# A second queue for the kept results of the first gate/up stage

## The chip, the cores and the metric

The kernel runs on one core of a Trainium2 chip. The metric is the device time of one execution in microseconds; the time before is the median of three runs. All data is float32. TensorE is called PE in the profile, its weight loads PEld, VectorE DVE, ScalarE ACT, GpSimd POOL and SyncE SP. Entries with a q (SPq, ACTq) belong to an engine's instruction queue, where its DMAs are issued, in order.

## What is computed

One decoder layer over 2048 rows of 1024: a mixing sub-layer (sliding-window attention beside a convolution group, then an output projection), and a SwiGLU channel mixer with 2816 inner channels. The change lies in the channel mixer:

```python
hn = rms_norm(h, ffn_pre_g)
ff = (jax.nn.silu(hn @ w_gate) * (hn @ w_up)) @ w_down
h = h + rms_norm(ff, ffn_post_g)
```

## The kernel before

The 2048 rows are worked on as four tiles of 512 rows. The channel mixer takes two tiles at a time: first the pair `ws = (0, 1)`, later the pair `ws = (2, 3)`. For each pair, `stage_pre` and `stage_p1` make the gate and up products and `stage_p2` the down product. The three stages of the first pair stand before those of the second, and between and beside them run lanes of other work: the attention of the last tile, the convolution taps (`fc@C`, VectorE), the output projection and norms (`stage_w`, `norm_w`), the preparation of operands (`stage_h_plain`, `stage_h_sums`) and, beside the first pair's `stage_p1`, differences of the down weights (`stage_tsums`, lines 1072 to 1086), which load and store through SP's queue and compute on VectorE.

The gate/up product is a two-by-two block product done by a scheme of seven products instead of eight. `STEPS` (line 869) lists them: index 0 is A11 times B11, 1 is S1 times T1, 2 is S2 times T2, 3 is A12 times B21, 4 is S3 times T3, 5 is S4 times B22, 6 is A22 times T4. The A operands are weight blocks and their sums (`sums`, line 971, on VectorE), the B operands activations and their sums. Every operand is split into a high and a low part, so that a product is twelve matmuls of 128 x 128 by 128 x 512 (`product`, line 874). The split of a weight block takes a copy on ScalarE (line 792) and a subtraction (line 796; on VectorE throughout the first pair).

`MATS` (line 872) lists 44 row blocks of weights, gate and up in turn. Of these, the first `PRE` (20 for the first pair, 16 for the second) have two of their seven products done early, in `stage_pre`, since the operands B11 and B21 need only the first tile of the pair. `stage_pre` runs over q from 0 to 2 x PRE: in the first half product A11 B11 of block m is copied out of PSUM by ScalarE into an `fa` tile (line 941) and stored to a DRAM array `keeps` (line 942, on ScalarE's queue, 256 KB each). In the second half the kept result is fetched (`fetch`, line 900, issued at q for q + 2), copied by ScalarE into a PSUM bank (`seed`, line 915, one product ahead) and product A12 B21 is accumulated onto it; the outcome is final for one quarter of the output and goes through silu or the product with the gate. The first eight q of the first pair are run inside `stage_w(1)`, the rest after it.

`stage_p1` then runs over all row blocks m. For a block with m < PRE the steps are 1, 2, 4, 5, 6, so it has five products (nst = 5, j counts them); the others have all seven. At j = 0 the kept result of A11 B11, loaded a second time, is copied into the PSUM bank "B" (line 1026), onto which step 2 accumulates at j = 1. Inside block m, `sums(m + 1)` are written at j = nst - 4, `fetch(m + 1)` at j = nst - 2 (line 1066) and the weight loads `loads(m + 2)` at j = nst - 1.

Buffers: `gb` has two, used by the kept results in both stages and by `y5` (line 1036) in `stage_p1`; `fa` has four, `raw` two, `chl` five; the PSUM tag `mm` has four banks. GpSimd does, in this stretch of the first pair, the attention's selects (line 494), the row norms' small operations (lines 153 to 156) and twelve of the low parts of T1, T3 and T4 in `stage_h_sums` (line 796).

The program's order is not what the engines follow to the letter: a scheduler takes the instructions by priority, in the order written, with a simulated time line, gives each tile a buffer when one is free, and fixes one order for each engine's queue at build time. At run time each queue goes in that order and every instruction waits for its own producers.

Of the kernel before, what the change touches and what calls it, by code (L numbers as in the profile page):

```python
# [37 lines left out]
def layer_kernel(ctx, tc, x, xT, cols, rows, sinks, relb, onehot, w_in, w_pw, w_out, w_gate, w_up, w_down, out):  # L38
    nc = tc.nc
# [15 lines left out]
    def t_(tag, shape, dt=F32):  # L55
        return sb.tile(list(shape), dt, tag=tag, name=nm(tag), bufs=BUFS[tag])
# [4 lines left out]
    def f2(tag, shape=(P, T)):  # L61
        return t_(tag, shape)

    def hl(tag):
        return t_(tag, (P, 2, T), F32R)
# [725 lines left out]
    def split_f(x, w):  # L791
        act(w[:, 0], x, AF.Copy)  # L792
        return w

    def lo(x, w, on_pool):
        (ptt if on_pool else vtt)(w[:, 1], x, w[:, 0].bitcast(F32), ALU.subtract)
# [77 lines left out]
    def product(o, w, op, first):  # L874
        n = 0
        for k in range(4):
            ks = slice(k * P, (k + 1) * P)
            for a, b in ((0, 0), (0, 1), (1, 0)):
                mat(o, w[:, a, ks], op[k][:, b], start=first and n == 0, stop=n == 11, skip_group_check=not first)
                n += 1  # L880

    def stage_pre(ws, ops, mid, keep, q0=0, q1=None):
        PRE = PRES[ws[0]]
        q1 = q1 or 2 * PRE
        L = f"F{ws[0]}"
        raws = {}
        wops = {}
        kept = {}

        def load(q):  # L890
            if q < q1 and q % 2 == 0:
                lab[0] = L
                half, m = divmod(q, PRE)
                raw = t_("raw", (P, 2, T))
                for j in range(2):
                    src, pr = MATS[m + j]
                    nc.sync.dma_start(raw[:, j], src[2 * pr][:, half * T : (half + 1) * T])
                    raws[q + j] = raw[:, j]

        def fetch(q):  # L900
            if PRE <= q < q1:
                lab[0] = L
                kept[q] = f2("gb")
                nc.sync.dma_start(kept[q], keep[q - PRE])

        def split(q):
            if q < q1:
                lab[0] = L
                raw = raws.pop(q)
                wops[q] = split_f(raw, hl("w"))  # L910
                lo(raw, wops[q], ws[0] and q % 2 == 1)

        seeded = {}

        def seed(q):
            if PRE <= q < q1:
                lab[0] = L
                seeded[q] = mm()
                act(seeded[q], kept.pop(q), AF.Copy)  # L919

        load(q0)
        load(q0 + 2)
        for q in range(q0, q0 + 3):
            split(q)
        for q in range(q0, q1):
            half, m = divmod(q, PRE)
            started.add(f"P{ws[0]}.{q}")
            bn = "B21" if half else "B11"
            if len(ops.get(bn, ())) < 4:
                lh.until(f"{bn}.{ws[0]}")  # L930
            split(q + 3)
            load(q + 4)
            fetch(q + 2)
            lab[0] = L
            seed(q + 1)
            lab[0] = L
            o = seeded.pop(q) if half else mm()
            product(o, wops.pop(q), ops[bn], not half)
            if not half:
                u = f2("fa")  # L940
                act(u, o, AF.Copy)
                nc.scalar.dma_start(keep[m], u)
            else:
                if MATS[m][0] is w_gate:
                    sg = f2("fa")
                    act(sg, o, AF.Silu)
                else:
                    vtt(sg, sg, o, ALU.mult)
                    nc.sync.dma_start(mid[0, MATS[m][1]], sg)
            yield 2.76  # L950

    def stage_p1(ws, ops, mid, keep):
        PRE = PRES[ws[0]]
# [7 lines left out]
        def loads(m):  # L961
            if m < len(MATS):
                lab[0] = L
                src, pr = MATS[m]
                r0 = t_("raw", (P, 2, T))
                nc.sync.dma_start(r0, src[2 * pr].rearrange("p (a b) -> p a b", a=2))
                r1 = t_("chl", (P, 2, T))
                nc.sync.dma_start(r1, src[2 * pr + 1].rearrange("p (a b) -> p a b", a=2))
                raws[m] = dict(A11=r0[:, 0], A12=r0[:, 1], A21=r1[:, 0], A22=r1[:, 1])

        def sums(m):
            if m < len(MATS):
                lab[0] = L
                r = raws[m]
                s12 = t_("chl", (P, 2, T))
                r["S1"], r["S2"] = s12[:, 0], s12[:, 1]
                vtt(r["S1"], r["A21"], r["A22"], ALU.add)
                vtt(r["S2"], r["S1"], r["A11"], ALU.subtract)
                s34 = t_("chl", (P, 2, T))
                r["S3"], r["S4"] = s34[:, 0], s34[:, 1]  # L980
                vtt(r["S3"], r["A11"], r["A21"], ALU.subtract)
                vtt(r["S4"], r["A12"], r["S2"], ALU.subtract)

        wops = {}
        kept = {}

        def split(q):
            if q < len(todo):
                m, j, i, n = todo[q]
                lab[0] = L  # L990
                wops[q] = split_f(raws[m][STEPS[i][1]], hl("w"))
                lo(raws[m][STEPS[i][1]], wops[q], ws[0] and i in POOL_LO)

        def fetch(m):
            if m < PRE:
                lab[0] = L
                kept[m] = f2("gb")
                nc.sync.dma_start(kept[m], keep[m])

        loads(0)  # L1000
        sums(0)
        for q in range(AHEAD):
            split(q)
        loads(1)
        fetch(0)
        sg = {}
        for q, (m, j, i, nst) in enumerate(todo):
            pre = m < PRE
            gate = MATS[m][0] is w_gate
            pr = MATS[m][1]  # L1010
            split(q + AHEAD)
            lab[0] = L
            which, an, bn = STEPS[i]
            if len(ops.get(bn, ())) < 4:
                lh.until(f"S{ws[0]}")
                lab[0] = L
            if j == 0:
                bk = {}
                if not gate:
                    blocks = {}  # L1020
                    if pre:
                        blocks[3] = f2("fa")
                        nc.sync.dma_start(blocks[3], mid[0, pr])
                if pre:
                    bk["B"] = mm()
                    act(bk["B"], kept.pop(m), AF.Copy)  # L1026
            first = which not in bk
            if first:
                bk[which] = mm()
            o = bk[which]  # L1030
            product(o, wops.pop(q), ops[bn], first)
            if i == 0:
                bk["B"] = mm()
                act(bk["B"], o, AF.Copy)
            elif i == 1:
                y5 = f2("gb")
                act(y5, o, AF.Copy)
            elif i == 2:
                x2 = f2("at")
                act(x2, o, AF.Copy)  # L1040
            else:
                v = {4: y5, 5: x2}.get(i, o)
                if v is not o:
                    vtt(v, v, o, ALU.add)
                if gate:
                    s = f2("fa")
                    act(s, v, AF.Silu)  # L1047
                    sg[i] = s
                else:
                    s = sg.pop(i)  # L1050
                    vtt(s, s, v, ALU.mult)
                    blocks[i] = s
                    if i in (3, 4, 6):
                        nc.sync.dma_start(mid[{3: 0, 4: 4, 6: 1}[i], pr], s)
                    if i == 5:
                        a11, a22, a21 = blocks[3], blocks[4], s
                        for to, o_, p_, op, q_ in ((5, a22, a21, ALU.add, a22), (3, a21, a11, ALU.subtract, a21),
                                                   (2, a11, a22, ALU.subtract, a11)):
                            (ptt if ws[0] else vtt)(o_, p_, q_, op)
                            nc.sync.dma_start(mid[to, pr], o_)  # L1060
                    if i == 6:
                        (ptt if ws[0] else vtt)(s, s, blocks[3], ALU.subtract)
                        nc.sync.dma_start(mid[6, pr], s)
            if j == nst - 4:
                sums(m + 1)
            if j == nst - 2:
                fetch(m + 1)
            if j == nst - 1:
                loads(m + 2)
            yield 2.76  # L1070
# [337 lines left out]
    ws, ops = (0, 1), {}  # L1408
# [12 lines left out]
    ws, ops = (2, 3), {}  # L1421
# [76 lines left out]
```

## Time and profile before

| what | us |
|---|---|
| median of 3 runs | 1991.65 |
| lowest and highest run | 1988.4, 1992.08 |
| profiled execution, device time | 1988.67 |
| its span, first to last instruction | 1986.6 |

The granted TensorE clock of that execution was 0.992 of full speed. The DMAs that the change touches, from the profile's list of issues:

```profile
gb@F<-keeps SPq DMA_DIRECT2D x72, 256.0 KB, 3.9
...
keeps<-fa@F ACTq DMA_DIRECT2D x36, 256.0 KB, 5.0
```

The last figure is the median time in microseconds from issue to landing. The rows are for both pairs: 40 of the 72 loads and 20 of the 36 stores belong to the first. A name like `gb@F` is a tile's tag with the stage in which it was made: A and B mixing, C convolution, W output projection, H operand preparation, F gate and up, G down, and G also the differences of the down weights. The bracket behind a line of the timeline holds the idle time before the instruction and what ended it.

### The profile page before, as it was taken

The page shows a single profiled execution, that of the slowest core. Times are in us where ns is not written, and L with a number is a line of the kernel's source. Part 1 is how long each engine was busy: PE and PEld are TensorE (multiplying, and loading weights), DVE is VectorE, ACT ScalarE, POOL GpSimd, SP SyncE. Part 2 cuts the span into 40 slices and gives each one's busy share as a digit, 9 for nine tenths or more (in the row PEclk, how much of TensorE's full clock was granted, in tenths as well). Part 3 has the DMA queues.
Part 4 walks back from the last instruction along what each step waited for, and adds up shares of the span by engine and source line. Part 5 has one row for each costly group of instructions (what it writes and reads, how often), then busy time and mean ns, then how long its engine had stood idle before and what let it go on. Part 6 is the DMA issues. An engine that isn't in the chain of part 4 may idle for free.

```text
span 1986.6 us, 26669 instructions
## 1 busy us (share of the span) xinstructions
PE 1930.2 (97%) x8730; PEld 1542.3 (78%) x8730; DVE 1460.2 (73%) x2578; ACT 955.2 (48%) x1878; POOL 336.4 (17%) x415
## 2 busy tenths in 40 slices
PE   8999999998999999899999999989999999999997
PEld 6777767776777778778888778768888888888886
DVE  5999969986875898888658975766666665455557
ACT  5455454436737633334355466556634433345443
POOL 4011111003121200000000110144423332311003
PEclk9999999999999999999999999989999999999999
DMA  8797757669659867885477788797844542466664
GB/s 312 253 316 234 228 176 242 213 198 306 203 191 353 290 216 237 285 267 181 154 236 251 266 302 282 270 315 244 289 149 165 170 164 81 143 232 194 210 196 144
DMA packets 229403, 454.56 MB, mean 229 GB/s; under 512 B 22632, under 2 KB 48400, under 8 KB 229264
## 3 DMA queue, kind: packets, MB, share of 16 engines
q1 hardware_dynamic: 211024, 426.64, 64.5%
q10 hardware_dynamic: 18240, 26.22, 3.6%
q8 instruction: 69, 1.13, 0.2%
q14 instruction: 70, 0.57, 0.1%
HBM read 331.65 MB, written 121.12 MB: 228 GB/s over the span
## 4 chain that ended last, share of the span: by engine, by line
PE 43%; DMA 10%; DVE 9%; issue 3%; POOL 2%; ACT 2%; SPq 1%; DVEq 0%; ACTq 0%; POOLq 0%
PE mm@F L85 29%; PE mm@G L85 12%; DVE fc@C L94 2%; PE tr@W L85 2%; DMA gb@F<-keeps 1%; DVE hl@G L94 1%; DMA mids<-fa@F 1%; DMA fa@G<-mids 1%; DMA td<-fc@G 1%; DVE w@F L94 1%; DMA fc@G<-w_down 1%; DMA wx@G<-w_down 1%; DVE fa@F L94 1%; DVE chl@F L94 1%; DMA mixT<-fc@C 1%
## 5 line engine op out<-in xcount | busy, mean ns | idle before, releaser
L94 DVE SCALAR_TENSOR_TENSOR fc@C<-glu@C,colt,fc@C 128x512 f32<-128x512 f32 x480 | 356.5, 760 | 2.9
L85 PE MATMUL mm@F<-hl@H,w@F 128*128 128x512 f32 x1056 | 253.0, 390 | 3.3 <-ACT mm@F L919 2.0
L85 PE MATMUL mm@G<-hl@G,hl@G 128*128 128x512 f32 x924 | 232.6, 397 | 11.2 <-ACT hl@G L792 7.7
L85 PEld LDWEIGHTS mm@F<-hl@H,w@F 128*128 128x128 f32 x1056 | 197.5, 188 | 46.3 <-ACT mm@F L919 3.7
L85 PEld LDWEIGHTS mm@G<-hl@G,hl@G 128*128 128x128 f32 x924 | 173.0, 190 | 51.7 <-ACT hl@G L792 9.0
L85 PE MATMUL mm@A<-hl@A,w@A 128*128 128x512 f32 x840 | 206.5, 395 | 4.2 <-ACT w@A L127 1.9
L792 ACT ACTIVATE w@F<-chl@F 128x512 fp32r<-128x512 f32 x220 | 135.4, 625 | 142.1 <-PE mm@F L85 131.5
L85 PE MATMUL mm@G<-w@G,hl@G 128*128 128x512 f32 x876 | 199.4, 389 | 0.0
L85 PEld LDWEIGHTS mm@G<-w@G,hl@G 128*128 128x128 f32 x876 | 164.4, 188 | 34.1
L85 PEld LDWEIGHTS mm@A<-hl@A,w@A 128*128 128x128 f32 x840 | 155.4, 188 | 42.2 <-ACT w@A L127 2.6
L94 DVE TENSOR_TENSOR w@F<-chl@F,w@F 128x512 fp32r<-128x512 f32 x198 | 144.8, 735 | 35.9 <-ACT w@F L792 35.3
L85 PE MATMUL mm@F<-ql@H,w@F 128*128 128x512 f32 x528 | 128.4, 391 | 9.2 <-ACT mm@F L1026 5.0
L85 PE MATMUL mm@F<-mid@H,w@F 128*128 128x512 f32 x528 | 131.7, 396 | 0.0
L85 PE MATMUL mm@F<-p@H,w@F 128*128 128x512 f32 x528 | 129.4, 390 | 0.0
L85 PE MATMUL mm@F<-x@H,w@F 128*128 128x512 f32 x528 | 125.7, 391 | 0.0
L85 PEld LDWEIGHTS mm@F<-ql@H,w@F 128*128 128x128 f32 x528 | 98.8, 188 | 31.6 <-ACT mm@F L1026 6.4
L494 POOL TENSOR_SCALAR_AFFINE_SELECT p@B<-p@B 128x512 f32<-128x512 f32 x62 | 57.6, 938 | 374.0 <-ACT p@B L492 372.7
L85 PEld LDWEIGHTS mm@F<-mid@H,w@F 128*128 128x128 f32 x528 | 100.0, 190 | 21.9 <-ACT fa@F L1047 0.5
L85 PEld LDWEIGHTS mm@F<-p@H,w@F 128*128 128x128 f32 x528 | 99.5, 188 | 21.0 <-ACT at@F L1040 0.2
L85 PEld LDWEIGHTS mm@F<-x@H,w@F 128*128 128x128 f32 x528 | 98.6, 188 | 21.5 <-issue 0.8
L127 ACT ACTIVATE w@A<-raw@A 128x512 fp32r<-128x512 f32 x110 | 67.4, 625 | 93.5 <-PE mm@A L85 54.8
L94 DVE TENSOR_TENSOR w@G<-raw@G,w@G 128x512 fp32r<-128x512 f32 x73 | 51.5, 705 | 68.1 <-ACT w@G L792 66.8
(302 smaller groups left out, 3300.6 us busy)
## 6 DMA issues: line engine op xcount, KB each, us to landing
mids<-fa@F SPq DMA_DIRECT2D x154, 256.0 KB, 2.8
raw@A<-w_in SPq DMA_DIRECT2D x55, 512.0 KB, 4.7
w@A<-lo_in SPq DMA_DIRECT2D x84, 256.0 KB, 3.6
fc@G<-mids SPq DMA_DIRECT2D x77, 256.0 KB, 3.5
fa@G<-mids SPq DMA_DIRECT2D x75, 256.0 KB, 4.6
gb@F<-keeps SPq DMA_DIRECT2D x72, 256.0 KB, 3.9
w@W<-fold SPq DMA_DIRECT2D x32, 512.0 KB, 5.1
chl@F<-w_gate SPq DMA_DIRECT2D x22, 512.0 KB, 4.1
```

Of the source, the lines that this page charges most:

```text
L85: r = nc.tensor.matmul(*args, **kw)
L94: r = op(*args, **kw)
L127: act(w[:, 0], raw, AF.Copy)
L494: nc.gpsimd.affine_select(out=pg[:, kb].rearrange("p (i q) -> p i q", q=P), in_=pg[:, 1].rearrange("p (i q) -> p i q", q=P), compare_op=AL ...
L792: act(w[:, 0], x, AF.Copy)
```

## The change

For the first pair of tiles (`ws[0]` is 0) three DMAs are issued by GpSimd: the store of the kept result in `stage_pre` (before on ScalarE's queue), its load in `stage_pre` and its load in `stage_p1` (both before on SP's queue). In `stage_p1` of the first pair, the load for block m + 1 is written at j = 1 instead of j = nst - 2, which is 3 for the blocks that have a kept result. For the second pair nothing changes. Sizes, buffers and arithmetic stay as they are.

```diff
@@ stage_pre, fetch
-                nc.sync.dma_start(kept[q], keep[q - PRE])
+                (nc.sync if ws[0] else nc.gpsimd).dma_start(kept[q], keep[q - PRE])
@@ stage_pre, first half
                 u = f2("fa")
                 act(u, o, AF.Copy)
-                nc.scalar.dma_start(keep[m], u)
+                (nc.scalar if ws[0] else nc.gpsimd).dma_start(keep[m], u)
@@ stage_p1, fetch
                 kept[m] = f2("gb")
-                nc.sync.dma_start(kept[m], keep[m])
+                (nc.sync if ws[0] else nc.gpsimd).dma_start(kept[m], keep[m])
@@ stage_p1
-            if j == nst - 2:
+            if j == (nst - 2 if ws[0] else 1):
                 fetch(m + 1)
```

## The prediction

> **What bounds the kernel now.** I read the page first: the span, and the chain of work that ended last.
>
> ```profile
> span 1986.6 us, 26669 instructions
> PE 1930.2 (97%) x8730; PEld 1542.3 (78%) x8730; DVE 1460.2 (73%) x2578; ACT 955.2 (48%) x1878; POOL 336.4 (17%) x415
> ...
> PE mm@F L85 29%; PE mm@G L85 12%; DVE fc@C L94 2%; PE tr@W L85 2%; DMA gb@F<-keeps 1%; DVE hl@G L94 1%; DMA mids<-fa@F 1%; DMA fa@G<-mids 1%; DMA td<-fc@G 1%; DVE w@F L94 1%; DMA fc@G<-w_down 1%; DMA wx@G<-w_down 1%; DVE fa@F L94 1%; DVE chl@F L94 1%; DMA mixT<-fc@C 1%
> ```
>
> TensorE is busy for 97% of the span, so a change can gain only where TensorE stands still. Where that is, the table of windows shows; its columns are stretch, length, then busy time and count for TensorE, its weight loads, VectorE, ScalarE and GpSimd, then the granted clock, the DMA share and the rate.
>
> ```profile
> 600.00:622.00 22.00, 22.00 (x99) 18.22 (x98) 13.39 (x19) 16.75 (x28) 2.88 (x12) 1.00 0.96 349
> 622.00:686.00 64.00, 60.53 (x276) 48.49 (x275) 47.06 (x66) 43.79 (x79) 16.72 (x12) 1.00 0.93 314
> 740.00:760.00 20.00, 20.00 (x90) 16.55 (x89) 20.00 (x34) 7.51 (x13) 0.00 (x0) 1.00 0.40 134
> 800.00:820.00 20.00, 14.33 (x56) 11.00 (x55) 17.95 (x30) 3.79 (x7) 0.00 (x0) 0.91 0.78 264
> 860.00:880.00 20.00, 16.21 (x66) 12.94 (x65) 17.63 (x30) 6.17 (x12) 0.00 (x0) 0.93 0.78 249
> 690.00:960.00 270.00, 256.54 (x1108) 209.00 (x1107) 228.39 (x367) 97.86 (x175) 0.00 (x0) 0.99 0.71 235
> 1050.00:1400.00 350.00, 339.01 (x1512) 275.57 (x1511) 253.00 (x412) 197.15 (x356) 67.57 (x92) 0.99 0.81 278
> ```
>
> The first gate/up stage has two parts that use kept results. In `stage_pre`'s second half (622 to 686 us) TensorE loses 64.00 - 60.53 = 3.5 us. In `stage_p1` (from 686 us on) it loses 270.00 - 256.54 = 13.5 us between 690 and 960, and two slices fall out: 56 and 66 matmuls where an undisturbed one has 90. The waits of 690 to 1000 us name ScalarE's copy of a kept result into PSUM (line 1026), which stands still for its load; the columns are total, times, longest.
>
> ```profile
> ACT mm@F L1026 <- DMA gb@F<-keeps: 60.4, 16, 11.7
> PEld mm@F L85 <- ACT mm@F L1026: 6.4, 4, 4.2
> PEld mm@F L85 <- ACT w@F L792: 4.5, 1, 4.5
> PEld mm@F L85 <- DVE gb@F L94: 4.0, 2, 2.1
> ```
>
> ScalarE's 60 us are mostly covered. What reaches TensorE is seen in the timelines around 711, 813 and 877 us:
>
> ```profile
> 711.60 1.45 PE L85 MATMUL mm@F<-ql@H,w@F 128*128 128x512 f32 x5 [1.23 <-ACT mm@F L1026]
> ...
> 796.02 0.60 ACT L1026 ACTIVATE mm@F<-gb@F 128x512 f32<-128x512 f32 x1 [3.16 <-DMA gb@F<-keeps]
> 796.72 0.63 SPq L1023 DMA_DIRECT2D fa@F<-mids  x1
> ...
> 803.93 1.66 PE L85 MATMUL mm@F<-yt@H,w@F 128*128 128x512 f32 x6 [1.65 <-DVE gb@F L94]
> ...
> 807.62 0.42 SPq L1054 DMA_DIRECT2D mids<-fa@F  x1
> 808.10 0.42 SPq L998 DMA_DIRECT2D gb@F<-keeps  x1
> 813.18 0.60 ACT L1026 ACTIVATE mm@F<-gb@F 128x512 f32<-128x512 f32 x1 [11.72 <-DMA gb@F<-keeps]
> 814.38 0.73 PE L85 MATMUL mm@F<-ql@H,w@F 128*128 128x512 f32 x2 [4.03 <-ACT w@F L792]
> ...
> 877.38 1.22 PE L85 MATMUL mm@F<-ql@H,w@F 128*128 128x512 f32 x2 [3.79 <-ACT mm@F L1026]
> ```
>
> The kept buffer was free from 796.6 us, when the copy before had read it, yet SP issued the next load at 808.10, after eight other DMAs of its queue in those 11.4 us, the first and the last of them shown. ScalarE takes its queue in order, so the weight splits behind line 1026 waited too, and TensorE with them.
>
> **What the change removes there.** The load of the next block is written after the second product instead of the fourth of five, on a queue that has nothing else to do: GpSimd is at 0.00 from 690 to 960 us. So the load can go when the buffer falls free, some 11 us sooner around 800 us. Price of the stalls, with a matmul at 20.00/90 = 0.222 us: 800 to 820 us lacks 34 matmuls, 7.6 us, of which 1.65 us was a wait for VectorE that stays: 5.9. 860 to 880 us lacks 24: 5.3. This counts the lower granted clock after the gap (0.91 and 0.93) along with the gap. With 1.23 us at 711 us: 12.4 us. I take 10, since VectorE is at 17.95 and 17.63 of 20 us in just these slices and TensorE waits for it elsewhere in this stretch (4.0 us); the next late thing is VectorE's work. Ends: 4 (VectorE takes most) and 12.4.
>
> **What it puts at risk in `stage_pre`.** Lines 904 and 942 change queue too.
>
> ```profile
> L904 SPq DMA_DIRECT2D gb@F<-keeps x18: 319/327/1285, 615.1 to 674.8; - x18
> ...
> DMA to landing us min/median/max: 3.4/5.4/6.5
> ...
> L998 SPq DMA_DIRECT2D gb@F<-keeps x19: 319/423/755, 692.6 to 949.6; - x19
> ...
> L942 ACTq DMA_DIRECT2D keeps<-fa@F x20: 326/326/1106, 531.8 to 626.2; - x20
> ...
> DMA to landing us min/median/max: 3.1/5.2/6.8
> ```
>
> Eighteen of the twenty second-half loads run from 615.1 to 674.8 us through two `gb` buffers: 59.7 x 2 / 18 = 6.6 us a turn. Landing takes 5.4 of it and the copy 0.6; 0.6 is slack and SP's delay. The chain of waits between 630 and 671 us is mostly these loads, one after the other, and a load goes as soon as the copy ends:
>
> ```profile
> 634.00 5.50 DMA gb@F<-keeps
> ...
> 648.67 5.88 DMA gb@F<-keeps
> ...
> 656.57 5.86 DMA gb@F<-keeps
> ...
> 667.43 3.38 DMA gb@F<-keeps
> ```
>
> ```profile
> 654.57 0.60 ACT L919 ACTIVATE mm@F<-gb@F 128x512 f32<-128x512 f32 x1 [1.63 <-DMA gb@F<-keeps]
> 655.20 0.32 SPq L904 DMA_DIRECT2D gb@F<-keeps  x1
> ```
>
> So what GpSimd's queue adds to a load, call it x, counts here: nine turns, each with 0.6 us of cover, cost 9 (x - 0.6). No DMA of GpSimd's is in the trace; the nearest rows are its work on tiles of the same 128 x 512:
>
> ```profile
> L494 POOL TENSOR_SCALAR_AFFINE_SELECT p@B<-p@B 128x512 f32<-128x512 f32 x62 | 57.6, 938 | 374.0 <-ACT p@B L492 372.7
> ...
> L796 POOL TENSOR_TENSOR p@H<-chl@H,p@H 128x512 fp32r<-128x512 f32 x4 | 6.1, 1527 | 7.1 <-ACT p@H L865 7.1
> ```
>
> Low end: the load leaves SP's backlog and lands like the quickest, 3.4 instead of 5.4, x = -2.0; TensorE can then win back at most the 3.5 us it loses. High end: it stands behind two of the twelve subtractions that GpSimd does in 622 to 686 us, x = 2 x 1.53 = 3.1, cost 22 us. I take x = 1.05, the select's 0.94 us and a tenth for standing behind the subtractions: 9 x 0.45 = 4 us. The subtractions in turn stand behind loads; the last of them has 17 us until TensorE first uses its result, which covers that:
>
> ```profile
> 666.92 1.74 POOL L796 TENSOR_TENSOR mid@H<-chl@H,mid@H 128x512 fp32r<-128x512 f32 x1
> ```
>
> ```profile
> 685.95 1.52 PE L85 MATMUL mm@F<-mid@H,w@F 128*128 128x512 f32 x6
> ```
>
> The Trainium skill ("DMA: Bandwidth & Descriptors", Specifications) puts the first byte at about 1 us for GpSimd's path and 0.6 for SP's. By that, an estimate, x would be 0.4, the cost here nothing and the profiled execution 1978.7 us; no run here shows it.
>
> **Stores and issue time.** ScalarE loses twenty issues of 0.33 us, 6.5 us, and SP forty of about 0.4; neither queue's time bounds TensorE where the stores are (22.00 of 22.00 us busy up to 622), so I cost these at 0. The store is covered by four `fa` buffers at one product each (12 x 0.222 = 2.7 us), 10.7 us against a landing of 5.2: if it stands over 5.5 us behind a select or a row norm on GpSimd, ScalarE stops at the next copy out, and then TensorE when its four banks are full. That price is in the rivals.
>
> **Sum.** -10 + 4 + 0 = -6 us against the profiled execution's own 1988.67 us (span 1986.6 and 2.1 around it): 1982.7. The median of the three runs shown is 1991.65, 3.0 higher; the forecast of a median is 1985.7 us, 0.3% faster. With the good ends, -12.4 - 3.5, it is 1975.8; with the bad one of `stage_pre`, -10 + 22, it is 2003.7.
>
> **Rivals**, each as a median.
> *Slower, by the two buffers.* GpSimd's issue is longer than I take it, and `stage_pre` runs at the pace of the kept loads. At x = 1.7 the ten microseconds are given back; from 2.15 on the kernel is slower by over 4 us; at 3.1 it is at 2003.7. For it: the chain above is already these loads, and GpSimd is busy 16.72 us there. Against: what SP's own queue adds to a turn goes.
> *Another wait takes its place.* VectorE or SP's weight loads hold `stage_p1` at nearly the same pace; gain 4, cost 4: 1991.7. For it: VectorE at 20.00 of 20.00 in 740 to 760 us. Against: TensorE has no gap in that very slice. The Trainium skill ("DMA: Bandwidth & Descriptors", Issuing engines are not separate DMA queues) points the same way: another issuing engine saves only the sequencer's time. The rows at 796 to 813 us bear that out only in part, as 11.5 of the 16.6 us from copy to copy are the wait for the issue, not for the transfer.
> *The loads get quicker everywhere* (x below 0.6): -10 - 3: 1978.7.
> *Queue order on GpSimd.* A store stands behind a select that waits for ScalarE, up to 21 us as the waits of 520 to 1000 us show,
>
> ```profile
> POOL p@B L494 <- ACT p@B L492: 54.3, 5, 21.4
> ```
>
> so 21.4 - 5.5 - three free banks (8.0) = 8 us, once; or the order of instructions, which is made anew at the build, falls worse later, bounded by doubling the 11 us that TensorE loses in 1050 to 1400 us. About +9: 1994.7, slower at the upper end.
> *The load doesn't move*, since its buffer is not free: excluded by 796.6 against 808.10.
>
> **Chances.** Forecast 0.46, two buffers 0.20, another wait 0.12, quicker loads 0.12, queue order 0.10. A measurement of this kernel tells about 0.2%, 4 us, from no change: faster means under 1987.7, slower over 1995.6. The forecast's own range, 1980 to 1990, gives two thirds to faster, a third to the same; with the quicker loads and a little of the others, faster 0.48, same 0.24, slower 0.28. The range is 1976 to 2004, its ends those of the unknown x.
>
> **What would show it.** Right: the wait of line 1026 for its load falls from 60 us to under 10, the 800 and 860 us slices are back at about 90 matmuls and a clock of 1.00, the load is issued within 3 us of the copy before it. The cost of `stage_pre`: the gap of TensorE between 622 and 686 us grows from 3.5 to about 7.5, and landing of line 904, counted from the end of the copy before, from 5.4 to about 6.5. Wrong: that landing over 8 us; waits of line 941 for `fa`; a gap of TensorE for VectorE in `stage_p1` that grows by what line 1026 lost.

## The result, and the profile after

| | before | after |
|---|---|---|
| median of 5 runs, us | 1990.02 (1988.4 to 1992.08) | 1998.56 (1996.45 to 2000.56) |
| ratio, 95% interval | | 1.0049 [1.0038, 1.0061] |
| span of the profiled execution, us | 1986.6 | 1996.9 |

The change makes the kernel slower by half a per cent. The time lies inside the range that was given, on the other side of the forecast.

Where it went is read from first and last starts. These rows of the line view of the kernel after give line, engine, operation, count, shortest, median and longest duration in ns, then first and last start in us:

```profile
L919 ACT ACTIVATE mm@F<-gb@F x20: 576/598/603, 612.8 to 684.4; 128x512 f32<-128x512 f32 x20
L1026 ACT ACTIVATE mm@F<-gb@F x20: 594/602/605, 687.9 to 966.0; 128x512 f32<-128x512 f32 x20
L1037 ACT ACTIVATE gb@F<-mm@F x21: 579/599/602, 693.5 to 989.5; 128x512 f32<-128x512 f32 x21
```

And of the kernel before:

```profile
L919 ACT ACTIVATE mm@F<-gb@F x20: 583/602/604, 614.5 to 680.5; 128x512 f32<-128x512 f32 x20
L1026 ACT ACTIVATE mm@F<-gb@F x20: 594/602/602, 682.4 to 954.0; 128x512 f32<-128x512 f32 x20
L1037 ACT ACTIVATE gb@F<-mm@F x21: 577/597/601, 688.9 to 983.0; 128x512 f32<-128x512 f32 x21
```

Two measures follow, used for every run below. The "twenty copies" of `stage_pre`, from the first start of line 919 to the end of its last (0.6 us), took 66.6 us and now take 72.2. The "way to the 20th copy" of `stage_p1`, from the first line 1037 to the last line 1026, took 954.0 - 688.9 = 265.1 us and now takes 272.5. The stage begins 4.6 us later and has lost 12.0 us by its 20th copy; 10.3 are left at the end of the span. (`MATS` has 22 entries, each of two of the 44 row blocks, and `PRE` counts entries: the 20 blocks with a kept result are nearly the whole stage.)

Both measures come from one profiled execution each, which can lie some microseconds from the run's median (5.7 below it in e6, 4.7 above it in e11). The second is the coarser one: e1, e5, e6, e10, e11 and e14 below leave the DMAs of `stage_p1` as before, and their ways still run from 259.9 to 271.7 us. So a difference of a few microseconds in it says nothing by itself.

The windows of the kernel after (columns as in the prediction) show the same for TensorE:

```profile
622.00:686.00 64.00, 56.27 (x250) 44.83 (x249) 39.60 (x58) 43.29 (x75) 26.36 (x30) 0.97 0.89 299
690.00:960.00 270.00, 253.46 (x1083) 204.62 (x1082) 223.26 (x359) 96.76 (x174) 9.32 (x17) 0.98 0.71 232
800.00:820.00 20.00, 14.72 (x64) 11.53 (x62) 12.81 (x21) 4.59 (x9) 0.55 (x1) 1.00 0.82 257
860.00:880.00 20.00, 19.98 (x89) 16.22 (x88) 16.57 (x28) 7.81 (x14) 1.10 (x2) 1.00 0.85 282
```

In `stage_pre` its gap grew from 3.5 to 7.7 us, in `stage_p1` from 13.5 to 16.5. The slice at 860 us is repaired, the one at 800 us is not, and over the whole stretch 25 matmuls fewer were done. The waits of 690 to 1000 us say why:

```profile
POOL gb@F L998 <- DVE fa@F L94: 143.9, 9, 19.0
POOL gb@F L998 <- ACT fa@F L1047: 120.3, 9, 21.1
ACT mm@F L1026 <- DMA gb@F<-keeps: 62.3, 17, 11.6
```

The copy waits for its load as long as before (60.4 then, 62.3 now), and GpSimd, with nothing else to do, waits for each load's buffer. What frees it is not the copy of the last kept result: it is line 1047 or VectorE's product, the last readers of `y5`. The timeline of the kernel after around 813 us:

```profile
810.00 0.68 DVE L94 TENSOR_TENSOR gb@F<-gb@F,mm@F 128x512 f32<-128x512 f32 x1
...
812.40 0.68 DVE L94 TENSOR_TENSOR fa@F<-fa@F,gb@F 128x512 f32<-128x512 f32 x1
...
813.38 0.55 POOL L998 DMA_DIRECT2D gb@F<-keeps  x1 [16.85 <-DVE fa@F L94]
...
819.08 0.60 ACT L1026 ACTIVATE mm@F<-gb@F 128x512 f32<-128x512 f32 x1 [11.62 <-DMA gb@F<-keeps]
...
820.28 0.73 PE L85 MATMUL mm@F<-ql@H,w@F 128*128 128x512 f32 x2 [3.57 <-ACT w@F L792]
```

VectorE adds to `y5` at 810.00 and reads it for the last time from 812.40 to 813.08; the load follows 0.3 us later, and the copy again holds back the splits that TensorE needs. In the kernel before it is the same: a kept result does not get the buffer of the one before it. From the third on, each load starts, in both traces, only after the last read of the `y5` of two blocks earlier.

### The profile page after: what moved, and what is told of

It reads as the page before. It is cut to its first block, busy times and chain, and to the rows that moved or that the text cites. A ratio compares the mean times of both kernels' runs of the same rounds, so it can differ in the third digit from the quotient of the medians.

```text
span 1996.9 us, 26735 instructions
## 1 busy us (share of the span) xinstructions
PE 1935.4 (97%) x8730; PEld 1544.6 (77%) x8730; DVE 1459.4 (73%) x2578; ACT 955.0 (48%) x1878; POOL 369.8 (19%) x475
## 4 chain that ended last, share of the span: by engine, by line
PE 64%; DMA 12%; DVE 11%; issue 8%; POOL 3%; ACT 2%; SPq 1%; DVEq 0%; ACTq 0%; POOLq 0%
PE mm@F L85 29%; PE mm@G L85 12%; PE mm@A L85 11%; PE mm@W L85 4%; DVE fc@C L94 3%; PE tr@B L85 3%; PE tr@W L85 2%; DVE hl@G L94 1%; DMA fc@C<-y_scr 1%; DMA fa@G<-mids 1%; DMA mixT<-fc@C 1%; DMA mids<-fa@F 1%; DMA td<-fc@G 1%; DMA chl@W<-x 1%; PE tr@B L491 1%
## 5 line engine op out<-in xcount | busy, mean ns | idle before, releaser
L85 PE MATMUL mm@G<-hl@G,hl@G 128*128 128x512 f32 x924 | 231.9, 396 | 11.3 <-ACT hl@G L792 7.4
```

The lines of the kernel that those rows point to most:

```text
L85: r = nc.tensor.matmul(*args, **kw)
```

## The experiments

All eighteen compute the full result. Each time is a median, each ratio that of its runs to runs of the kernel before on the same chip, with a 95% interval; the ratio is worked out from the single runs and is not the quotient of the medians. The medians of before were 1987.6 to 1988.7 us. The last two columns are the measures defined above, each from the run's own profile.

| run | us | ratio | twenty copies | to the 20th copy |
|---|---|---|---|---|
| e1 stage_pre's store and load | 1992.35 | 1.0017 [1.0002, 1.0032] | 73.3 | 262.0 |
| e2 stage_p1's load, at j = 1 | 1990.10 | 1.0013 [0.9996, 1.0029] | 66.9 | 268.2 |
| e3 the change, y5 apart | 1999.03 | 1.0051 [1.0035, 1.0066] | 74.9 | 267.7 |
| e4 before, y5 apart | 1983.84 | 0.9971 [0.9957, 0.9985] | 66.9 | 253.8 |
| e5 e1 with ScalarE's order pinned | 1992.85 | 1.0030 [1.0017, 1.0043] | 75.4 | 259.9 |
| e6 stage_pre's load | 1997.94 | 1.0053 [1.0035, 1.0072] | 71.8 | 269.0 |
| e7 e4, load at j = 1 on SP | 1984.29 | 0.9983 [0.9970, 0.9995] | 67.5 | 254.5 |
| e8 e4, some lows on GpSimd | 1995.35 | 1.0040 [1.0026, 1.0054] | 69.1 | 269.0 |
| e9 the change, row norm on VectorE | 1998.82 | 1.0051 [1.0037, 1.0064] | 73.2 | 267.7 |
| e10 before, row norm on VectorE | 1995.89 | 1.0031 [1.0021, 1.0040] | 68.0 | 271.7 |
| e11 stage_pre's store | 1994.55 | 1.0030 [1.0020, 1.0041] | 68.8 | 269.2 |
| e12 e4, load at j = 1 on GpSimd | 1993.01 | 1.0029 [1.0013, 1.0045] | 65.8 | 267.1 |
| e13 the change in the order of before | 1993.82 | 1.0024 [1.0015, 1.0033] | 72.7 | 266.9 |
| e14 before in the order of the change | 1995.89 | 1.0035 [1.0022, 1.0047] | 70.8 | 268.7 |
| e15 e12 in the order of e7 | 1990.52 | 1.0009 [0.9998, 1.0020] | 66.7 | 260.7 |
| e16 e6 in the order of before | 1989.41 | 0.9998 [0.9988, 1.0008] | 69.5 | 267.1 |
| e17 e11 in the order of before | 1988.94 | 0.9999 [0.9988, 1.0010] | 69.4 | 265.5 |
| e18 e2 in the order of before | 1991.47 | 1.0008 [0.9996, 1.0019] | 66.5 | 267.8 |

**First: which stage, and which buffer.** e1 takes the first two hunks of the change alone, e2 the other two; e3 and e4 give `y5` another tag, in the change and in the kernel before.

```diff
# e1: lines 904 and 942 as in the change, lines 998 and 1066 as before
# e2: lines 998 and 1066 as in the change, lines 904 and 942 as before
# e3 (on the change), e4 (on before)
-                y5 = f2("gb")
+                y5 = f2("gb" if ws[0] else "at")
```

> Only stage_pre's store and load go to GpSimd; stage_p1 as before. Own theory (the change loses about 4 us in stage_pre and 6 in stage_p1, for different reasons): 3 to 6 us slower than before, TensorE's gap between the first kept copy and the start of stage_p1 up by about 4 us, and stage_p1 as long as before. Rival one (GpSimd's queue makes each load slower): the same loss, but with landing plus issue delay of line 904 longer by over 0.5 us than before. Rival two (the order made anew at the build decides, whatever is edited): any sign, within 8 us, with the load's turn no longer than before.

> Only stage_p1's load goes to GpSimd and to the second product; stage_pre as before. Own theory (the load waits for the buffer of y5, so its place in the program doesn't move it, and ScalarE's copy stands earlier in its queue and blocks the weight splits): 4 to 7 us slower than before, line 1026 still waits 50 us or more, loads still released by y5's consumer. The prediction's view (the load goes when the copy before has read its buffer): 8 to 12 us faster, line 1026 waits under 10 us. Rival two: any sign.

> The changed kernel with y5 of the first stage in an at buffer, so that gb holds kept results alone. Own theory: the load is now free when the copy of two blocks before has read the buffer; line 1026 waits under 10 us in stage_p1, and the kernel is 6 to 14 us faster than the changed one, about 4 faster to 4 slower than before. Rival one (GpSimd's queue is slow): still 6 to 10 us slower than before. Rival two: any sign, with stage_p1's length not following the waits of line 1026.

> The kernel before with y5 of the first stage in an at buffer; loads on SP's queue at the fourth product. Own theory: the load is free of y5, but still stands in SP's queue at the fourth product, so line 1026 still waits some 20 to 50 us; 0 to 5 us faster than before. If the buffer alone was what made line 1026 wait: 8 to 12 us faster, line 1026 under 10 us.

Each half alone costs little. e4 is faster than both kernels without any change of queue. Its waits in `stage_p1`:

```profile
ACT mm@F L1026 <- DVE at@F L94: 36.2, 10, 7.9
...
ACT mm@F L1026 <- DMA gb@F<-keeps: 0.8, 2, 0.4
```

The wait for the load is gone, from 60 us to 0.8, although the load stands where it always stood, on SP's queue behind the fourth product. With the load on GpSimd at j = 1 and the buffer still shared, 49.8 us of the wait are left in e2 and 53.7 in e18. So it was the shared buffer, far more than queue or place, that held it. Over half of the wait came back under another name: the copy's PSUM bank is freed by VectorE's addition. That is also why the way to the 20th copy flatters the runs with `y5` apart: the copy itself goes earlier. In e4 it is 11.3 us shorter than in the kernel before, but the 20th line 1037 starts only 4.3 us earlier (959.7 against 964.0). In e3 the load is as free (3.2 us of waiting) and nothing is gained; its `stage_pre` is the slowest but one, and its way to the 20th copy 14 us longer than e4's.

**Second: stage_pre.** e5 is e1 with the copies of line 919 and the 24 operand copies on ScalarE tied to the order that they have before; e6 moves the load alone, e11 the store alone. e9 and e10 take the row norm's inverse roots (lines 153 to 156) off GpSimd.

```diff
# e5 (on e1): the order edge that is set from each of the copies to the next in before's order
+            tc.add_manual_dep(pin[y], pin[x].name, NoSync)
# e6: line 904 as in the change, all else as before; e11: line 942 likewise
# e9 (on the change), e10 (on before), in norm_w
-        r = rsqrt(ssq, 4, D, w < 3)
+        r = rsqrt(ssq, 4, D, w not in (1, 3))
-        r2 = rsqrt(ssq2, 4, D, w < 3)
+        r2 = rsqrt(ssq2, 4, D, w not in (1, 3))
```

> stage_pre's store and load on GpSimd as in the run with these alone, but on ScalarE the twenty copies of line 919 and the 24 operand copies of stage_h_sums are tied to the order that they have in the kernel before. Order theory: the loss lies in where the rebuilt order puts these copies, so with it pinned TensorE's gap between 622 and 686 us falls from 8.8 to about 4 us, stage_p1 begins within 2 us of 688.9, landed to copy falls from 1.6 to about 0.6 us; time 1.0000 of before, give or take 0.0015. Queue theory (GpSimd's queue delays the loads): the gap stays near 8 us and the turn near 6.9 us whatever the order, 1.002 or more.

> Of stage_pre only the load goes to GpSimd, the store stays on ScalarE's queue. If the loss of stage_pre (TensorE gap 3.5 to 8.8 us with both moved) comes with the load: gap about 8 us again, 1.0015 to 1.003. If it comes with the store, which also takes twenty issues of ScalarE away and so lets the order be made anew before the loads begin: gap about 3.5 us, 1.000.

> The changed kernel, but the row norms' inverse roots of the first pair's second tile (lines 153 to 156 at 590 to 620 us) on VectorE instead of GpSimd, so that they no longer stand between the stores and loads of GpSimd's queue. Norm theory (the loss of stage_pre is that these twelve small operations now stand behind stores and loads, 9.0 us from first to last instead of 3.8, and the normed rows and all operands made from them come later): the first line 781 starts within 6 us of the last line 774 instead of 11, TensorE's gap in 622 to 686 us is at most 5 us, stage_p1 begins near 689; time 1.003 of before or less against 1.005 of the change. Rival (the kept loads themselves or ScalarE's order): the gap of 622 to 686 stays near 8 us.

> Control: the kernel before with the same inverse roots on VectorE. Nothing stands between them on GpSimd there, so nothing is to be won: 1.000 within 0.0015, gap of 622 to 686 us near 3.5, stage_p1 from about 689.

> Of stage_pre only the store goes to GpSimd. Norm theory: the stores alone stretch the row norm's chain to 8 us or more (they are issued once per product and wait for ScalarE's copy), last line 774 to first line 781 takes 8 us or more, TensorE's gap in 622 to 686 us is 6 us or more, 1.001 to 1.003. Rival (the loads make the loss): gap near 3.5 us, 1.000.

ScalarE's order alone is not the cause: pinned, the twenty copies take 75.4 us. The norm theory looked good in the timeline of GpSimd after the change, where twelve operations that took 3.8 us before (612.17 to 615.95) take 9.0, with three stores and two loads among them:

```profile
611.07 0.19 POOL L153 TENSOR_TENSOR sm@W<-sm@W 128x4 f32<-128x4 f32 x1 [2.08 <-DVE sm@W L94]
611.35 0.20 POOL L154 TENSOR_TENSOR sm@W<-sm@W,sm@W 128x4 f32<-128x4 f32 x1
612.38 0.56 POOL L942 DMA_DIRECT2D keeps<-fa@F  x1 [0.84 <-ACT fa@F L941]
...
618.76 0.58 POOL L904 DMA_DIRECT2D gb@F<-keeps  x1 [1.35 <-ACT mm@F L919]
619.37 0.42 POOL L155 TENSOR_SCALAR sm@W<-sm@W 128x4 f32<-128x4 f32 x1
619.88 0.20 POOL L156 TENSOR_TENSOR sm@W<-sm@W,sm@W 128x4 f32<-128x4 f32 x1
```

It fell all the same. In e9 the last line 774 is followed by line 781 after 2.6 us instead of 11, and TensorE's gap stays at 7.1 us, the twenty copies at 73.2. e10 gave something not asked for: moving a few tiny operations in the kernel before, where nothing was to be won or lost, costs 1.0031. e6 says that the load alone brings the slow twenty copies. The time does not follow TensorE's gap in 622 to 686 us, though: the gap is 8.8 us in e1 at a ratio of 1.0017, and 5.0 in e6 at 1.0053. The waits of e6, and those of the kernel after, hold one that is 0.2 us before: SP's load of `hT` waits for GpSimd's subtraction, and what is prepared from it stands ahead of the copies on ScalarE. The row is that of SP's queue in 618 to 692 us, after the change:

```profile
SPq L845 <- POOL p@H L796: 5.4, 2, 3.4
```

**Third: stage_p1 with y5 apart.**

```diff
# e7 (on e4), and e12 (on e4) with line 998 as in the change besides
-            if j == nst - 2:
+            if j == (nst - 2 if ws[0] else 1):
# e8 (on e4)
-                lo(raws[m][STEPS[i][1]], wops[q], ws[0] and i in POOL_LO)
+                lo(raws[m][STEPS[i][1]], wops[q], i in POOL_LO)
```

> y5 in the tag at, and the load of stage_p1 written at j = 1, on SP's queue; no DMA on GpSimd. Theory (with y5 apart the load is early enough at its old place, and VectorE and SP's weight loads set the pace): same as y5 apart alone, 0.997 within 0.0015, line 1026's wait for the load under 4 us in both, for DVE at@F 30 to 50 us. Rival (the earlier place is still worth something once the buffer is free): 0.994 or less. Second rival (an earlier load stands in front of weight loads on SP's queue and delays VectorE): 0.9985 or more, VectorE's waits for chl@F<-w_gate over 15 us.

> y5 in the tag at, loads as before, and in the first pair the weight low parts of steps 3 and 6 are subtracted by GpSimd instead of VectorE (one of five in the first twenty blocks), as the second pair has it. If VectorE's own work holds stage_p1 once the buffer is apart: TensorE's gap from the first line 1037 to the 20th copy falls from 9.2 to 5 us or less, 0.995 or less. If VectorE only waits for SP's weight loads: the gap stays near 9 us and the time at 0.997. If GpSimd's slower subtraction (about 1.4 us against 0.69) is on the path: slower than 0.998.

> The kernel before with y5 in the tag at, and the load of stage_p1 on GpSimd's queue at j = 1; stage_pre untouched. If stage_p1's part of the change is harmless by itself once the buffer is free, and the 14 us that y5 apart lost with the change against y5 apart without it come from the late operands of stage_pre: stage_p1 begins near 689, its 20th copy 254 us later, 0.998 or less. If GpSimd's loads cost in stage_p1: the 20th copy 262 us or more after the start, 1.001 or more.

With the buffer free, the earlier place is worth nothing (e7 as e4: VectorE, GpSimd and SP do their other work in the same order in both, and the loads are issued 24 us ahead of their copies in both). The other queue costs: e12's way to the 20th copy is 12.6 us longer than e7's, though its loads are issued 26 us ahead of their copies in the mean. What differs is that VectorE waits longer for weight loads of SP's queue. The groups of VectorE's operations in e7, 690 to 945 us, then in e12; the last part is idle time before them and what ended it:

```profile
L94 DVE TENSOR_TENSOR chl@F<-chl@F 128x512 f32<-128x512 f32 x18 | 12.4, 691 | 16.7 <-DMA chl@F<-w_gate 11.2 <-DMA chl@F<-w_up 5.4
...
L94 DVE TENSOR_TENSOR wx@G<-wx@G 128x512 f32<-128x512 f32 x10 | 6.9, 690 | 5.4 <-DMA wx@G<-w_down 5.0 <-issue 0.3
```

```profile
L94 DVE TENSOR_TENSOR chl@F<-chl@F 128x512 f32<-128x512 f32 x18 | 12.5, 692 | 23.7 <-DMA chl@F<-w_gate 15.6 <-DMA chl@F<-w_up 8.1
L94 DVE TENSOR_TENSOR wx@G<-wx@G 128x512 f32<-128x512 f32 x10 | 6.9, 691 | 10.7 <-DMA wx@G<-w_down 9.8 <-issue 0.8
```

These two groups alone have 7.0 + 5.3 = 12.3 us more idle time. That this makes the 12.6 us is read from its size; no run changes it alone. e8's subtractions took 1.58 us each on GpSimd against 0.69 on VectorE, and the run lost; whether by that or by its new order it does not say.

**Fourth: queue or order.** Such an edit lets the scheduler fix new orders: in the trace of the change, TensorE, ScalarE, VectorE and SP do much of the same work in another order than before. The last six runs part the two: after the whole program is written, each instruction of an engine is tied to its neighbour in the order of another build, without a wait, except the DMAs whose engine differs.

```diff
# e13: the change, held to the order of before; e14: before, held to the order of the change
# e15: e12 held to e7; e16: e6, e17: e11, e18: e2, each held to before
+    for first, second in zip(order[engine], order[engine][1:]):
+        tc.add_manual_dep(second, first.name, NoSync)
```

> The changed kernel with its three DMAs on GpSimd, and on all five engines every other instruction held in the order that it has in the kernel before; only the sixty DMAs of the change stand where the scheduler puts them. Order theory (the change loses because the rebuilt order of the queues is worse, not by what GpSimd's queue does to a transfer): 1.000 of before within 0.0015, lines 919's first to twentieth copy in 69 us or less, stage_p1 to its 20th copy about 265 us. Queue theory (GpSimd's in-order queue costs: loads behind its other work and that work behind loads): 1.003 or more, twenty copies in 71 us or more as in all six runs with this load on GpSimd.

> The reverse: the kernel before with its DMAs on SP's and ScalarE's queues and the load of stage_p1 at its old place, every other instruction held in the order of the changed kernel. Order theory: as slow as the change, 1.004 or more, the twenty copies of line 919 in 71 us or more. Queue theory: 1.000 to 1.0015, twenty copies in 69 us or less.

> y5 apart with the load of stage_p1 on GpSimd at j = 1, every other instruction in the order of the run with the same place on SP's queue; only the engine that issues these twenty loads differs. Order theory: the 12.6 us that the same change of queue lost in stage_p1 when the order was made anew (254.5 to 267.1 us to the 20th copy, VectorE's idle time 35 to 48) do not come, 256 us or less and 0.9985 or less of before. Queue theory (loads issued by GpSimd take something from the weight loads whatever the order): 263 us or more.

> Only stage_pre's load on GpSimd, all else in the order of the kernel before. Order theory: 69 us or less for the twenty copies of line 919, TensorE's gap in 622 to 686 us about 3.5 us, 1.000. Queue theory, with the ring that the waits of the load-only run suggest (SP's load of hT at line 845 waits for GpSimd's subtraction, which stands behind a kept load, which waits for a copy): 71 us or more, SP's wait at line 845 for GpSimd over 4 us, 1.002 or more.

> Only stage_pre's store on GpSimd, every other instruction in the order of the kernel before. The load alone in that order cost nothing (0.9998). If the 0.0024 that the whole change costs in the old order come with the stores, which stand between the row norm's small operations: 1.001 to 1.002, last line 774 to first line 781 over 6 us against 4.9. If they come with the load of stage_p1: 1.000 within 0.001, and the run of stage_p1's load shows them.

> Only the load of stage_p1 on GpSimd and at j = 1, y5 and the kept results still in the same two buffers, every other instruction in the order of the kernel before. The load cannot move, since its buffer is y5's: line 1026 waits 60 us or more in all. If GpSimd's issue, 0.3 us after the wait and 0.55 long, costs on each of these loads: 1.001 to 1.002, stage_p1 to its 20th copy 267 us or more against 265. If not: 1.000 within 0.001.

In the traces of all six, VectorE, GpSimd and SP do their other work exactly in the order that they are held to. Neither pure theory holds. The order of the change on the old queues costs 1.0035, the new queues in the old order 1.0024, both together 1.0049. The intervals of the first two overlap, so which of them is larger is not shown. The windows of e13 and then of e14 show a gap in each, 5.5 and 5.9 us, between before's 3.5 and the change's 7.7:

```profile
622.00:686.00 64.00, 58.54 (x259) 46.37 (x258) 41.11 (x61) 43.11 (x76) 30.24 (x33) 0.97 0.93 308
```

```profile
622.00:686.00 64.00, 58.10 (x253) 46.27 (x252) 39.95 (x59) 44.92 (x77) 16.49 (x12) 0.95 0.91 302
```

For the single moves it is the order. Held, the load alone goes from 1.0053 to 0.9998 and the store alone from 1.0030 to 0.9999, and SP's wait at line 845 for `p@H` falls from 6.3 to 0.2 us with the load; stage_p1's load goes from 1.0013 to 1.0008, within what the intervals can tell. In e17 the last line 774 is followed by line 781 after 7.2 us instead of 4.9, and this cost nothing, so the norm theory fails here too. TensorE's gap in 622 to 686 us is 5.0 us in e16 and 5.1 in e17: a gap there, too, can be made up later. e15 came out between its branches: holding the order gives back 6.4 of the 12.6 us (260.7 against 267.1 and 254.5); the other half stays with the queue. The ratios say the same (1.0009 against 1.0029 and 0.9983).

What the three moves cost together in the old order, 0.0024, looks like more than their sum (-0.0002 - 0.0001 + 0.0008 = 0.0005), but with about 0.001 of uncertainty in each of the four the difference is not clear of noise. The twenty copies of `stage_pre` show no such excess: they take 2.8 us more with the store on GpSimd, 2.9 with the load and 6.1 with all. What the 0.0024 consist of stays open. Stores and loads then stand in one queue, and the stores wait for line 941, the loads for line 919; whether a load is late because a store ahead of it waits, no run separates.

## Why the prediction was wrong

**The -10 us of `stage_p1`** is the step that failed, and with it the sign. It said: "The kept buffer was free from 796.6 us, when the copy before had read it", and took the 11.5 us to the issue at 808.10 for a delay on SP's queue. That was assumed from the tag's two buffers and not looked up. The timeline of the kernel before has the answer between two of the lines that were quoted:

```profile
805.60 0.69 DVE L94 TENSOR_TENSOR fa@F<-fa@F,gb@F 128x512 f32<-128x512 f32 x1
```

This is the last read of a `y5`, in that buffer, until 806.29. SP issued the load 1.8 us later, and those 1.8 are all that a queue could have saved. Over the eighteen loads from the third on, SP issued 1.2 us after such a last read in the mean (0.03 to 4.6), GpSimd after the change 0.3 each time. SP's waits of 690 to 960 us named the reader too:

```profile
SPq L998 <- ACT fa@F L1047: 5.3, 6, 2.5
```

The rival that "the load doesn't move, since its buffer is not free", excluded by 796.6 against 808.10, is what happened. In place of a gain of 10, the span lost 10.3 - 4.6 = 5.7 us from the start of `stage_p1` on; how much of that is the new order and how much the queue, the profiles do not part (e10, which leaves the DMAs of `stage_p1` alone, loses 4 us there). What the freed load is worth was over-sized as well: e4 gains 0.0029, some 6 us (3 to 9 by its interval), not 10 to 12, and VectorE is the next late thing, as the text had it. Even that is not the buffer's alone for certain: e4 and e7 share a new order of the queues, and no run has `y5` apart in the order of before.

**The +4 us of `stage_pre`** had the right size (stage_p1 begins 4.6 us later, the gap is 7.7 us where 7.5 was forecast) and the wrong cause. That the size fits is luck. The load was to be x = 1.05 us longer on GpSimd. These rows are the loads and stores of the first pair after the change, the loads in 612 to 690 us:

```profile
L904 POOL DMA_DIRECT2D gb@F<-keeps x18: 548/556/596, 613.6 to 679.2; - x18
...
DMA to landing us min/median/max: 2.8/4.9/6.8
```

```profile
L942 POOL DMA_DIRECT2D keeps<-fa@F x20: 542/558/768, 529.6 to 626.7; - x20
...
DMA to landing us min/median/max: 2.4/5.5/7.0
```

The loads land in 4.9 us where SP's took 5.4, the stores in 5.5 against 5.2. Over the eighteen loads from copy to copy, the mean time from the copy's end to the issue is 0.42 us (0.49 before), from issue to landing 4.86 (5.07, over the fifteen that have a landing in the trace): x is about -0.3. What grew is the time from landing to the copy, 0.56 to 1.59 us. Load and buffer were ready, and ScalarE was not. This growth goes with the order more than with the queue: it is 1.66 us in e14, with the loads on SP's queue in the order of the change, and 0.88 in e13, with the loads on GpSimd in the order of before. The held load alone costs nothing. By the figures of the Trainium skill ("DMA: Bandwidth & Descriptors", Specifications) the first byte would come 0.4 us later on GpSimd's path, an estimate; in these landings it does not show.

**The subtractions that stand behind loads** were priced at nothing, because the last of them has 17 us until TensorE needs it. They are also the last readers of a `chl` buffer that SP's load of `hT` waits for (5.4 us after the change). Whose buffer a delayed instruction frees was not asked. What that wait costs is not shown: in e13 it is 0.2 us, and the time is still 1.0024.

**The stores at 0** were right for the store alone (0.9999, held). That stores and loads share one queue was not in the sum.

**The queue order** had a chance of 0.10 and a price of about +9 us. It is a large part of what was measured: 0.0035 of 1988.65 is 7.0 us alone, beside 0.0024 or 4.8 us for the queues alone; the two do not add up, as together they are 0.0049. It was counted as an accident. In this kernel it is a price that an edit can easily have: of the twelve runs before the whole order was held, ten lay at 1.0013 or above, among them the control e10, and only e4 and e7, which removed a real wait and left every operation on its engine, were faster. Most of the ten move work as well; e14, which moves none, shows the order alone.

**Against what was said would show it:** line 1026's wait did not fall below 10 us, the 800 us slice has 64 matmuls, the load is issued 9.0 us after the end of the copy before it in the mean (0.3 to 14.7). No landing, counted from the copy before, is over 8 us (the longest of the kernel before was 8.9), and line 941 waits for no `fa` buffer: the two-buffers rival, with its long issue, did not occur. One sign did: TensorE's weight loads wait for VectorE's `gb@F` 9.2 us in 690 to 1000, against 4.0 before, although line 1026 lost nothing of its wait. That another wait takes the place of the one removed is seen where it could be, in e3 and e4.

## What to carry to other kernels

Before a transfer is called late, find the last reader of the very buffer that it writes, also when that reader belongs to another tile of the same tag; here another tag for one tile took away a wait that a queue and an earlier place could not. When the queues' order is made anew by a scheduler, compare an edit also with the order held: here, the two moves of `stage_pre` that had cost 0.3 and 0.5% then cost nothing that could be measured. An engine that looks idle has an in-order queue of its own, and what is put behind a waiting DMA there can be what frees a buffer for another engine.

## What the runs showed of the hardware that was not expected

GpSimd starts a DMA about 0.3 us after what it waits for has ended, in all eighteen loads of `stage_p1` from the third on, as in the timeline above (813.08 to 813.38), where SP's followed by 0.03 (655.17 to 655.20), and is taken up for 0.55 us by it against SP's 0.33. After that nothing is slower: 4.9 us to landing against 5.4 in `stage_pre`, the medians of the kernels after and before. The Trainium skill ("DMA: Bandwidth & Descriptors", Issuing engines are not separate DMA queues) says that another issuing engine does not add a path for the data; with the order held, the single moves at 0.9998, 0.9999 and 1.0008, none of them faster, agree.
